# Output projection as seven block products, merge by pairs of row tiles, later modulations in attention

## The chip, the cores and the metric

The kernel runs on one core of a Trainium2 chip. The metric is the device time of one execution in microseconds (us); lower is better. Three runs of the kernel before gave a median of 2693.46 us. TensorE (PE in the profile) does the matrix products, VectorE (DVE), ScalarE (ACT) and GpSimd (POOL) the elementwise work, and SyncE's queue (SPq) issues most of the transfers from HBM.

## The reference

One layer over 1024 latent tokens (width 1024), with 256 context tokens that latent queries attend to. All of it is in fp32:

```python
x  = x + 0.5*ml[2] * swiglu(modulate(rms_norm(x, norm1_g), ml[0], ml[1]), ffn1_w_in, ffn1_w_out)
hx = modulate(rms_norm(x, norm2_g), ml[3], ml[4])
bg, cg, vc, q, k, v, gt = split(hx @ w_in)              # ctx gives k, v too
y_conv = bg * short_conv(cg * vc, conv_w)
o      = latent_attention(rope(norm(q)), k_all, v_all)  # 8 query heads, 2 kv heads of 128
g_conv, g_attn = split(sigmoid(gt))
x = x + ml[5] * ((g_conv*(y_conv @ w_bc) + g_attn*(o @ w_ba)) @ w_out)     # merge, output projection
x = x + 0.5*ml[8] * swiglu(modulate(rms_norm(x, norm3_g), ml[6], ml[7]), ffn2_w_in, ffn2_w_out)
return rms_norm(x, final_g)
```

`ml = split(silu(c) @ w_mod + b_mod)` are nine modulation vectors of 1024; each costs a pass over a 1024 x 1024 weight.

## The kernel before

**Products.** All activations lie transposed: 128 channels on the partitions, tokens along the free axis, in two halves of 512 tokens, C0 and C1. An fp32 product is made of three fp32r matmuls (`mm3`): both factors are cut by `split` into a high part (ACT makes the copy `hi`) and a low part (`src - hi`, on DVE unless another engine is named), and high x high, high x low and low x high are summed in one PSUM bank (`ps`, five banks).

**Block products.** The class `Winograd` multiplies 2x2 blocks with seven products in place of eight. A pair is two groups of 128 output channels. For each pair products 1 and 2 come first (`first`, `start`), then 6, 7, 4 (`second`), then 5 and 3 (`third`); each is 4 row tiles x 3 matmuls = 12 matmuls of 128x512. Its left-hand sides are sums of weight blocks (tiles `s`, summed on POOL, then split into tiles `wl`); its right-hand sides are kept split as tiles `r` by `keep`. Both FFNs and the mix `hx @ w_in` use it; the output projection does not. For the second FFN (`fast`), the generator `norm0` makes the normalised right-hand sides of half C0 (products 1, 2 and 3 read them) and `norm1` those of C1 and the mixed ones. Nine pairs (`AH3`) of products 1 and 2 run ahead, and behind them `second` starts, which needs the norm of C1.

**The stretch around the change.** Attention runs over 16 units (8 heads x 2 halves); each unit makes scores, exponentials, transposes (`pt`, turned into split tiles `pts`) and value products (`po`). `merge(j, ch)` then makes one row tile j of the merged branches for one half: 24 matmuls over the 8 heads, a gate multiply, an add, a split into `mh`/`ml`. There are 16 merges. The output projection loops over the halves and over eight output tiles d: `load_cols(w_out, d)` loads and splits 512 KB of weights, 24 matmuls follow, and x is updated. During the eight C1 tiles the C0 norm of FFN2 runs beside them (`first`, the generator of `norm0`).

**Later modulations.** `later_mod(6)` and `later_mod(7)` (the generator `late_steps`, 76 steps) load 256 KB tiles `rawm` of `w_mod`; DVE adds each, times one number of silu(c), into `macc` (32 such multiply-adds), and a split, a one-row product and a transpose end each half. Before, four steps run behind each of 14 merges and four behind each C0 tile of the projection.

**Order.** The source order is a priority; a scheduler with a timeline model sets the order of instructions on each engine. All instructions are issued by one helper, so the profile's line is always L90 and its groups are told apart by tile names. Buffers are rings: `raw` 3 x 512 KB, `wh` and `wl` 4 each, `ps` 5 banks; a transfer into a ring slot waits until the slot's last reader is done.

Of the kernel before, what the change touches and what calls it, by code (L numbers as in the profile page):

```python
# [9 lines left out]
F32 = mybir.dt.float32  # L10
# [8 lines left out]
P = 128  # L19
# [32 lines left out]
def tile_dit_layer(  # L52
# [29 lines left out]
    class Engine:  # L82


        def __init__(self, engine):
            self.engine = engine
# [36 lines left out]
    def ps_s(n=512):  # L123
        return psum.tile([P, 512], F32, tag="s", name=uniq("ps"), bufs=5)[:, :n]
# [362 lines left out]
    class Winograd:  # L487
# [3 lines left out]

        def __init__(self, xs, gain, mod, m, pairs, plain=False, ahead=3, side_from=None):
# [12 lines left out]
            self.source, self.ready = self.lefts(pairs, side_from), []  # L507

        def keep(self, i, k, src, lo_eng=None):

# [102 lines left out]
        def lefts(self, pairs, side_from):  # L613
# [29 lines left out]
            for j, (wa, wb) in enumerate(pairs):  # L643
# [16 lines left out]
                if side_from is not None and j == side_from - 1:  # L660
                    for wa, wb in pairs[:side_from]:
                        yield from map(parts, cols(wa) + cols(wb))

        def prefetch(self, n, lo_engines=(None, None)):
# [26 lines left out]
        def first(self):  # L691

            u, c = ttile("u"), ttile("c")
            act.copy(out=u, in_=self.product(1))
            dve.tensor_add(out=c, in0=u, in1=self.product(2))
            return u, c

        def start(self, norm):

# [807 lines left out]

    o_parts = [None] * NQ  # L1510

    def split_output(hd, *chunks):
        if o_parts[hd] is None:
            o_parts[hd] = atile("oh", dt=F32R), atile("ol", dt=F32R)
        a, b = chunks[0][1], chunks[-1][1] + 512
        split(q_f[hd][:, a:b], *(t[:, a:b] for t in o_parts[hd]))

    class Unit:
        def __init__(self, hd, ch):
# [82 lines left out]
            value()  # L1602
            yield

    m_hi, m_lo = {}, {}
    wa = {}

    def merge(j, ch):

        if j not in m_hi:  # L1610
            m_hi[j], m_lo[j] = atile("mh", dt=F32R), atile("ml", dt=F32R)
# [7 lines left out]
        terms = [  # L1619
            (w[0][:, k], w[1][:, k], *(t[:, o : o + 512] for t in o_parts[k])) for k in range(KD)  # L1620
        ]
# [5 lines left out]
        dve.tensor_add(out=ga, in0=ga, in1=z)  # L1627
# [43 lines left out]
    run(fill)  # L1671
    run(rest, 4)
    split_output(NQ - 2, C0, C1)
    split_output(NQ - 1, C0)
    merges = (step for j in range(2) for step in merge(j, C0))
    for _ in rest:
        run(merges, 2)
    run(merges)
    split_output(NQ - 1, C1)


    for j in range(KD):
        for ch in (C0, C1):
            if (j, ch) not in ((0, C0), (1, C0)):
                run(merge(j, ch))
                run(late_steps, 4)
    xs = Latents("x2")
    fast = Winograd(xs, None, modl, 6, column_pairs(ffn2_w_in[0], ffn_offsets), ahead=AH3)
    first = fast.norm0()
    for ch in (C0, C1):  # L1690
        o = ch[1]
        for d in range(KD):
            w = load_cols(w_out[0], d * P)
            load(xs(d, ch), xd[d, :, o : o + 512])
            ps = ps_s()
# [3 lines left out]
            dve.scalar_tensor_tensor(  # L1699
                out=xs(d, ch), in0=ps, scalar=modl[:, 40 + d : 41 + d], in1=xs(d, ch), op0=ALU.mult, op1=ALU.add  # L1700
            )
            if ch == C0:
                run(late_steps, 4)
                if d == KD - 1:
                    fast.gain = norm_gain("gain3", 6, "g3")["l"]
# [142 lines left out]
```

## Time and profile before

| what | before |
|---|---|
| median of 3 runs (lowest to highest) | 2693.46 us (2692.87 to 2695.69) |
| profiled execution, its own time | 2692.97 us |
| its span, mean granted TensorE clock | 2691.1 us, 0.995 |
| PE busy | 2646.4 us, 98% |
| DVE busy | 2016.0 us, 75% |
| ACT busy | 1178.8 us, 44% |
| POOL busy | 513.8 us, 19% |
| HBM traffic over the span | 138 GB/s |

The profile records one execution. Views used below: the totals by engine; groups of instructions by tile (count, busy us, mean ns, idle time before them and what ended it); stretches of the span with the busy time of each engine, the granted clock (PEclk, 1.00 is full speed) and the DMA share; the chain of work that ended last; and the timeline of one engine, a row for each run of like instructions (start, length, count, and in brackets the idle time before it with what ended it).

### The profile page before, as it was taken

Reading aid. Unit: us, or ns where it says so; the run is one execution under the profiler, and the core shown is the slowest. Engines: PE = TensorE matmul, PEld = TensorE weight load, DVE = VectorE, ACT = ScalarE, POOL = GpSimd, SP = SyncE. Lnnn points to the kernel's source line nnn. Section 1 sums busy time; section 2 is a strip of 40 time slices with the busy share of each in tenths; the row PEclk is TensorE's granted clock in tenths of the full one; section 3 lists DMA queues with packets and bytes.
Section 4 is the critical chain, followed back from the end, with each engine's and each line's share of the span. In section 5 each row is a group of like instructions: output and inputs, shape, how many; then the busy total and the mean of one; then the engine's idle time right before and its main releaser. Section 6 shows DMA issues by size and latency. Waiting matters only on the chain.

```text
span 2691.1 us, 36996 instructions
## 1 busy us (share of the span) xinstructions
PE 2646.4 (98%) x13437; PEld 2228.1 (83%) x13437; DVE 2016.0 (75%) x3363; ACT 1178.8 (44%) x2324; POOL 513.8 (19%) x403
## 2 busy tenths in 40 slices
PE   8999999999999999999999999999999999999998
PEld 5787899888778878888999888877888788888888
DVE  5788966888887899877487666785658886667885
ACT  6523454433454633333245666664236333334453
POOL 0144201221010044333023111000001442321200
PEclk9999999999999999999999999999999999999999
DMA  8565465346974345332213311011733552327841
GB/s 317 196 204 176 146 215 173 117 126 215 286 179 122 111 155 180 108 111 94 80 48 105 112 48 44 28 52 59 246 119 129 180 168 87 95 86 278 192 91 63
DMA packets 368206, 372.68 MB, mean 138 GB/s; under 512 B 18822, under 2 KB 257560, under 8 KB 368024
## 3 DMA queue, kind: packets, MB, share of 16 engines
q1 hardware_dynamic: 359000, 353.03, 39.9%
q0 software_dynamic: 9024, 17.30, 4.0%
q8 instruction: 105, 1.72, 0.3%
q14 instruction: 77, 0.63, 0.1%
HBM read 302.59 MB, written 67.63 MB: 138 GB/s over the span
## 4 chain that ended last, share of the span: by engine, by line
PE 91%; DVE 4%; DMA 2%; issue 2%; ACT 1%; POOL 0%; SPq 0%; DVEq 0%; POOLq 0%; ACTq 0%
PE ps L90 75%; PE pt L90 8%; PE po L90 7%; DMA rawm<-in_w_mod_dram 1%; DVE r L90 1%; DVE macc L90 0%; DMA ws<-in_ffn_w_out_dram 0%; DVE wl L90 0%; DVE nt L90 0%; DMA raw<-in_ffn_w_in_dram 0%; POOL s L90 0%; DVE uc L90 0%; DVE y L90 0%; DVE m L90 0%; DVE ol L90 0%
## 5 line engine op out<-in xcount | busy, mean ns | idle before, releaser
L90 PE MATMUL ps<-r,wl 128*128 128x512 f32 x5196 | 1206.5, 391 | 10.3 <-DVE wl L90 4.2
L90 PEld LDWEIGHTS ps<-r,wl 128*128 128x128 f32 x5196 | 974.1, 189 | 219.3 <-DVE wl L90 6.3
L90 ACT CAST wl<-s 128x512 fp32r<-128x512 f32 x254 | 156.7, 619 | 321.2 <-PE ps L90 218.7
L90 POOL TENSOR_TENSOR s<-raw 128x512 f32<-128x512 f32 x64 | 94.4, 1474 | 1051.2 <-DMA raw<-in_ffn_w_in_dram 630.7
L90 ACT CAST wl<-raw 128x512 fp32r<-128x512 f32 x287 | 177.5, 619 | 215.3 <-PE ps L90 153.9
L90 DVE TENSOR_TENSOR wl<-raw,wl 128x512 fp32r<-128x512 f32 x287 | 201.9, 705 | 62.1 <-ACT wl L90 60.3
L90 DVE TENSOR_TENSOR wl<-s,wl 128x512 fp32r<-128x512 f32 x254 | 230.4, 908 | 19.9 <-ACT wl L90 18.5
L90 POOL TENSOR_TENSOR s<-raw,s 128x512 f32<-128x512 f32 x64 | 103.8, 1623 | 361.1 <-DVE wl L90 361.1
L90 DVE SCALAR_TENSOR_TENSOR macc<-rawm,silu_c,macc 128x512 f32<-128x512 f32 x178 | 148.7, 852 | 25.0 <-DMA rawm<-in_w_mod_dram 24.3
L90 PE MATMUL ps<-wh,r 128*128 128x256 f32 x768 | 141.6, 285 | 0.0
L90 DVE TENSOR_TENSOR pts<-pt,pts 128x512 fp32r<-128x512 f32 x160 | 108.6, 686 | 41.4 <-ACT pts L90 40.2
L90 DVE TENSOR_TENSOR u<-u,ps 128x512 f32<-128x512 f32 x174 | 118.0, 678 | 27.8 <-PE ps L90 27.7
L90 ACT CAST pts<-pt 128x512 fp32r<-128x512 f32 x160 | 92.8, 592 | 89.5 <-PE pt L90 87.9
L90 DVE TENSOR_REDUCE m<-ps 128x1 f32<-128x512 f32 (+1 forms) x192 | 110.9, 595 | 26.0 <-PE ps L90 24.9
L90 ACT CAST rh<-hid 128x512 fp32r<-128x512 f32 x132 | 81.2, 620 | 107.1 <-PE ps L90 90.4
L90 PE MATMUL ps<-rh,wl 128*128 128x512 f32 x360 | 122.4, 390 | 2.8 <-ACT rh L90 2.8
L90 PEld LDWEIGHTS ps<-wh,r 128*128 128x128 f32 x768 | 120.6, 192 | 0.0
L90 PE MATMUL po<-pts,vh 128*128 128x512 f32 x256 | 111.7, 443 | 1.5 <-ACT pts L90 1.4
L90 PE MATMUL ps<-wl,r 128*128 128x256 f32 x384 | 108.8, 283 | 0.0
L90 PE MATMUL ps<-kl,qs 128*128 128x512 f32 x384 | 106.2, 397 | 0.4 <-ACT pc L90 0.4
L90 DVE TENSOR_TENSOR rl<-hid,rh 128x512 fp32r<-128x512 f32 x132 | 89.9, 684 | 21.7 <-PE ps L90 12.0
L90 ACT CAST wh<-raw 128x512 fp32r<-128x512 f32 (+1 forms) x85 | 67.9, 801 | 84.1 <-PE ps L90 57.7
(312 smaller groups left out, 5100.7 us busy)
## 6 DMA issues: line engine op xcount, KB each, us to landing
raw<-in_ffn_w_in_dram SPq DMA_DIRECT2D x130, 512.0 KB
raw<-in_ffn_w_out_dram SPq DMA_DIRECT2D x72, 512.0 KB
rawm<-in_w_mod_dram SPq DMA_DIRECT2D x136, 256.0 KB
raw<-in_w_in_dram SPq DMA_DIRECT2D x61, 512.0 KB
hid<-hd SPq DMA_DIRECT2D x40, 512.0 KB
ws<-in_ffn_w_out_dram POOLq DMA_DIRECT2D x30, 512.0 KB, 6.5
ucd<-uc SPq DMA_DIRECT2D x25, 512.0 KB
hd<-c SPq DMA_DIRECT2D x40, 256.0 KB
```

The lines of the kernel that those rows point to most:

```text
L90: inst = getattr(self.engine, name)(*args, **kw)
```

## The change

**The output projection** becomes a fourth use of `Winograd` (`proj`), with four pairs, output tiles i and i + 4. `lefts_apart` is the new list of left-hand sides: it makes 28 parts from 20 loads of 512 KB of `w_out`, with 24 sums on POOL, and gives every fourth part's low half to POOL. `start_all` runs products 1 and 2 of all four pairs, `second_of` products 6, 7 and 4 of each, and `third` products 5 and 3: 28 products of 12 matmuls. `add2` updates x and makes its squares. Half C0 of x is complete only when the last `second_of` is done, so `norm0` of FFN2 runs beside `third`.

**The merge** goes by pairs of row tiles (i, i + 4), C0 ahead of C1, and itself makes and keeps the seven right-hand sides (sums on DVE, one on POOL); the low halves of `w_ba` go to POOL. The attention outputs are kept split as one tile `op` for each head and half.

**Later modulations**: two steps run at two places of each of 15 attention units, three behind each merge outside attention and behind each step of the projection's first two phases; the gain of norm 3 is made ahead of the third phase.

```diff
     def split_output(hd, *chunks):
-        a, b = chunks[0][1], chunks[-1][1] + 512
-        split(q_f[hd][:, a:b], *(t[:, a:b] for t in o_parts[hd]))
+        for ch in chunks:
+            t = o_parts[hd, ch] = atile("op", (P, 2, 512), F32R)
+            split(q_f[hd][:, ch[1] : ch[1] + 512], t[:, 0], t[:, 1])
...
+        def lefts_apart(self, pairs):
...
+            for wa, _ in pairs:
+                yield from map(parts, halves(wa))
+            for wa, wb in pairs:
+                a, b = halves(wa), halves(wb)
+                s2, s3 = ttile("s2"), ttile("s3")
+                pool.tensor_add(out=s2, in0=b[0], in1=b[1])
+                pool.tensor_sub(out=s2, in0=s2, in1=a[0])
+                pool.tensor_sub(out=s3, in0=a[0], in1=b[0])
+                yield parts(s2)
+                yield parts(s3)
+                yield parts(b[1])
+            for wa, wb in pairs:
+                a, b = halves(wa), halves(wb)
+                s1, s2 = ttile("s1"), ttile("s2")
+                pool.tensor_add(out=s1, in0=b[0], in1=b[1])
+                pool.tensor_sub(out=s2, in0=s1, in1=a[0])
+                pool.tensor_sub(out=s2, in0=a[1], in1=s2)
+                yield parts(s1)
+                yield parts(s2)
...
     def merge(j, ch):
...
-            wa[j] = load_cols(w_ba[0], j * P)
+            wa[j] = load_cols(w_ba[0], j * P, pool)
...
-        split(ga, m_hi[j][:, o : o + 512], m_lo[j][:, o : o + 512])
+        if ch == C0:
+            out = raw_m[i][:, lower]
+            dve.tensor_add(out=out, in0=ga, in1=z)
+            proj.keep(1 + lower, i, out)
+        elif not lower:
+            dve.tensor_add(out=ga, in0=ga, in1=z)
+            dve.tensor_sub(out=t1, in0=ga, in1=raw_m[i][:, 0])
+            proj.keep(5, i, t1)
+        else:
+            dve.tensor_sub(out=t1, in0=ga, in1=t1)
+            pool.tensor_sub(out=b12, in0=ga, in1=b12)
...
             if n == 2:
                 run(fill, 1)
+                run(late_steps, 2)
...
-    for ch in (C0, C1):
-        for d in range(KD):
-            w = load_cols(w_out[0], d * P)
-            mm3(ps, [
-                (w[0][:, k], w[1][:, k], m_hi[k][:, o : o + 512], m_lo[k][:, o : o + 512]) for k in range(KD)
-            ])
-            if ch == C1:
-                fast.square(d)
-                if d in (0, 1):
-                    run(first, 1)
-                if d == 2:
-                    run(first)
+    proj.start_all(lambda: run(late_steps, 3))
+    for i, t in enumerate(proj.started):
+        add2(i, C0, t[:, 1])
+        add2(i + 4, C0, proj.second_of(t))
+        run(late_steps, 3)
+    run(late_steps)
+    fast.gain = norm_gain("gain3", 6, "g3")["l"]
+    for i, t in enumerate(proj.started):
+        run(first, 1 if i < 3 else None)
+        u, v = proj.third(t[:, 0], t[:, 1])
+        add2(i, C1, u)
+        add2(i + 4, C1, v)
```

**The order on the engines.** Three places. First PE, at the norm of half C0 for FFN2: `rs_y` is the reciprocal root that four matmuls spread over the partitions (`pt`), behind which DVE makes the right-hand sides `r`; in the rows of before, `mh`, `ml`, `wh`, `wl` are the output projection's factors. Before:

```order
L90 MATMUL pt_18980<-ident,rs_y_18931 128x128 x4
L90 MATMUL ps_19073<-mh_18434,wh_19067 128x512
L90 MATMUL ps_19073<-ml_18435,wh_19067 128x512
L90 MATMUL ps_19073<-mh_18434,wl_19068 128x512
L90 MATMUL ps_19109<-mh_17742,wh_19103 128x512
L90 MATMUL ps_19109<-ml_17743,wh_19103 128x512
```

The same place after the change; tiles `r_33` and `r_34` are right-hand sides of the projection, `r_3540` to `r_3542` the first of FFN2:

```order
L90 MATMUL pt_19172<-ident,rs_y_19106 128x128 x4
L90 MATMUL ps_19319<-r_3364_18248,wl_19228 128x512 x2
L90 MATMUL ps_19319<-r_3394_18419,wl_19228 128x512 x3
L90 MATMUL ps_19319<-r_3421_18582,wl_19228 128x512 x3
L90 MATMUL ps_19334<-r_3340_18121,wl_19276 128x512 x3
L90 MATMUL ps_19334<-r_3371_18294,wl_19276 128x512 x3
L90 MATMUL ps_19334<-r_3401_18465,wl_19276 128x512 x3
L90 MATMUL ps_19334<-r_3428_18628,wl_19276 128x512 x3
L90 MATMUL ps_19377<-r_3540_19183,wl_19363 128x512 x3
L90 MATMUL ps_19377<-r_3541_19188,wl_19363 128x512 x3
L90 MATMUL ps_19377<-r_3542_19193,wl_19363 128x512 x3
```

Before, 75 projection matmuls stand between the spread and FFN2's first product; after, 20 do.

Second PE again, at the norm of half C1: between this spread and the first of FFN2's products 6, 7 and 4 (on tiles that this norm makes). Before, the last rows ahead of that product and its first row:

```order
L90 MATMUL ps_19701<-r_3484_19011,wl_19634 128x512
L90 MATMUL ps_19701<-r_3485_19016,wl_19634 128x512 x3
L90 MATMUL ps_19701<-r_3486_19021,wl_19634 128x512 x3
L90 MATMUL ps_19701<-r_3487_19026,wl_19634 128x512 x3
L90 MATMUL ps_19722<-r_3549_19371,wl_19661 128x512 x2
```

After:

```order
L90 MATMUL ps_19850<-r_3555_19258,wl_19783 128x512
L90 MATMUL ps_19850<-r_3556_19263,wl_19783 128x512 x3
L90 MATMUL ps_19850<-r_3557_19268,wl_19783 128x512 x3
L90 MATMUL ps_19850<-r_3558_19273,wl_19783 128x512 x3
L90 MATMUL ps_19871<-r_3605_19520,wl_19810 128x512 x2
```

The spread stands 148 matmuls ahead of that product before and 111 ahead of it after (`pt_19302` and `pt_19451`), since fewer of the nine pairs' products are left when C1 of x is complete.

Third DVE, near the end of attention: `pts` are the split transposes that the value products wait for, `macc` the multiply-adds of the later modulations. Before:

```order
L90 TENSOR_TENSOR pts_17097<-pt_17092,pts_17097 128x512
L90 SCALAR_TENSOR_TENSOR macc_3284_17932<-rawm_17978,silu_c,macc_3284_17932 128x512
L90 SCALAR_TENSOR_TENSOR macc_3284_17932<-rawm_17981,silu_c,macc_3284_17932 128x512
L90 TENSOR_REDUCE rsum_17446<-rs_17625 128x1
L90 RECIPROCAL rinv_17888<-rsum_17446 128x4
L90 SCALAR_TENSOR_TENSOR macc_3284_17932<-rawm_17984,silu_c,macc_3284_17932 128x512
L90 TENSOR_TENSOR pts_17136<-pt_17131,pts_17136 128x512
```

After:

```order
L90 TENSOR_TENSOR pts_17717<-pt_17712,pts_17717 128x512
L90 TENSOR_SCALAR macc_3251_17678<-rawm_17679,silu_c 128x512
L90 TENSOR_TENSOR modl<-mcol_17675,bcol 128x4
L90 TENSOR_TENSOR pts_17728<-pt_17723,pts_17728 128x512
L90 SCALAR_TENSOR_TENSOR macc_3251_17678<-rawm_17790,silu_c,macc_3251_17678 128x512
L90 TENSOR_TENSOR pts_17739<-pt_17734,pts_17739 128x512
L90 SCALAR_TENSOR_TENSOR macc_3251_17678<-rawm_17793,silu_c,macc_3251_17678 128x512
```

Where three multiply-adds stood together ahead of a `pts`, now at most one does, and 24 of the 32 stand further up, between the transposes of attention.

More of the change, by code (lines that the diff above doesn't have):

```diff
@@ L487, in tile_dit_layer, with __init__ @@
     class Winograd:
-        def __init__(self, xs, gain, mod, m, pairs, plain=False, ahead=3, side_from=None):
+        def __init__(self, xs, gain, mod, m, pairs, plain=False, ahead=3, side_from=None, apart=False):
             self.xs, self.gain, self.mod, self.m, self.plain = xs, gain, mod, m, plain
@@ L506, in __init__ @@
             self.n_squares, self.accs = {}, {}
[L507 removed]
+            self.source, self.ready = (self.lefts_apart(pairs) if apart else self.lefts(pairs, side_from)), []
         def keep(self, i, k, src, lo_eng=None):
@@ L662, in lefts, with halves, parts @@
                         yield from map(parts, cols(wa) + cols(wb))
+        def lefts_apart(self, pairs):
+            def halves(src):
+                t = wpool.tile([P, SLOT], F32, tag="raw", name=uniq("raw"), bufs=3)
+                load(t[:].rearrange("p (k n) -> p k n", n=P), src.rearrange("(k p) n -> p k n", p=P))
+                return t[:, :512], t[:, 512:]
+            n_parts = [0]
+            def parts(src):
+                n_parts[0] += 1
+                t = wpool.tile([P, 2, 512], F32R, tag="wl", name=uniq("wl"), bufs=W_BUFS)
+                split(src, t[:, 0], t[:, 1], pool if n_parts[0] % 4 == 0 else None)
+                return t
+            for wa, _ in pairs:
[17 more added lines that the diff above has]
+                yield parts(s2)
         def prefetch(self, n, lo_engines=(None, None)):
@@ L696, in first, with start_all, second_of @@
             return u, c
+        def start_all(self, after=lambda: None):
+            for _ in range(self.n_ahead):
+                t = wpool.tile([P, 2, 512], F32, tag="wh", name=uniq("uc"), bufs=W_BUFS)
+                act.copy(out=t[:, 0], in_=self.product(1))
+                dve.tensor_add(out=t[:, 1], in0=t[:, 0], in1=self.product(2))
+                self.started.append(t)
+                after()
+        def second_of(self, t):
+            u, v, b = t[:, 0], t[:, 1], ttile("b")
+            dve.tensor_add(out=u, in0=u, in1=self.product(6))
+            dve.tensor_add(out=v, in0=u, in1=self.product(7))
+            dve.tensor_sub(out=b, in0=v, in1=self.product(4))
+            return b
         def start(self, norm):
@@ L1603, in seconds @@
             yield
-    m_hi, m_lo = {}, {}
-    wa = {}
+    wa, raw_m = {}, {}
+    proj = Winograd(
+        None, None, None, 0, [(w_out[0][:, i * P : (i + 1) * P], w_out[0][:, (i + 4) * P : (i + 5) * P]) for i in range(4)],
+        ahead=4, apart=True,
+    )
     def merge(j, ch):
-        if j not in m_hi:
-            m_hi[j], m_lo[j] = atile("mh", dt=F32R), atile("ml", dt=F32R)
+        i, lower = j % 4, j // 4
         if j not in wa:
-            wa[j] = load_cols(w_ba[0], j * P)
+            wa[j] = load_cols(w_ba[0], j * P, pool)
         w, o = wa[j], ch[1]
@@ L1674, in tile_dit_layer @@
     split_output(NQ - 1, C0)
-    merges = (step for j in range(2) for step in merge(j, C0))
+    merges = (step for j in (0, 4) for step in merge(j, C0))
     for _ in rest:
@@ L1679, in tile_dit_layer @@
     split_output(NQ - 1, C1)
-    for j in range(KD):
+    for i in range(4):
         for ch in (C0, C1):
-            if (j, ch) not in ((0, C0), (1, C0)):
-                run(merge(j, ch))
-                run(late_steps, 4)
+            for j in (i, i + 4):
+                if (i, ch) != (0, C0):
+                    run(merge(j, ch))
+                    run(late_steps, 3)
     xs = Latents("x2")
```

37 lines of the change are left out of this document (20 added, 17 removed).

## The prediction

> **What bounds the kernel now.** I read the totals by engine first, then the chain that ended last, then stretches of the span around the change.
>
> ```profile
> PE 2646.4 (98%) x13437; PEld 2228.1 (83%) x13437; DVE 2016.0 (75%) x3363; ACT 1178.8 (44%) x2324; POOL 513.8 (19%) x403
> PE 91%; DVE 4%; DMA 2%; issue 2%; ACT 1%; POOL 0%; SPq 0%; DVEq 0%; POOLq 0%; ACTq 0%
> ```
>
> PE is busy for 98% of the span and carries 91% of the chain. So a matmul taken away is worth its full time, unless something else is then late. The stretches (attention up to 1846, then merges, projection with the C0 norm, and the products ahead of FFN2's `second`):
>
> ```profile
> core 0: us, PE busy (x) PEld busy (x) DVE busy (x) ACT busy (x) POOL busy (x), PEclk, DMA share, GB/s
> 1440.00:1550.00 110.00, 109.63 (x590) 92.40 (x589) 78.90 (x169) 66.38 (x165) 27.27 (x27) 1.00 0.33 106
> 1750.00:1800.00 50.00, 48.25 (x276) 39.40 (x275) 44.22 (x93) 38.82 (x100) 0.00 (x0) 1.00 0.16 48
> 1800.00:1846.00 46.00, 40.32 (x224) 31.72 (x223) 28.53 (x43) 22.64 (x40) 0.00 (x0) 0.93 0.08 24
> 1870.00:1940.00 70.00, 70.00 (x310) 57.48 (x309) 46.50 (x69) 18.35 (x25) 0.00 (x0) 1.00 0.64 206
> 1940.00:2030.00 90.00, 90.00 (x404) 74.16 (x403) 54.98 (x85) 35.93 (x50) 0.00 (x0) 1.00 0.46 144
> 2030.00:2093.00 63.00, 61.40 (x279) 50.28 (x278) 54.23 (x86) 35.88 (x62) 12.04 (x7) 1.00 0.46 150
> ```
>
> Merges and projection (1870 to 2030) leave PE no idle time at all. PE waits at two places: the end of attention, and the end of the C1 norm (2030 to 2093, DVE busy 54.23 of 63).
>
> **The change part by part.** Sums are made against the profiled execution, 2692.97; the median is 0.5 above it.
>
> *Matmuls.* The projection's 384 matmuls become 28 products of 12, 336.
>
> ```profile
> L90 PE MATMUL ps<-mh,wl 128*128 128x512 f32 x128 | 49.9, 390 | 0.0
> L90 PE MATMUL ps<-mh,wh 128*128 128x512 f32 x128 | 49.9, 390 | 0.0
> L90 PE MATMUL ps<-ml,wh 128*128 128x512 f32 x128 | 49.8, 389 | 0.0
> 1918.29 27.23 PE ps L90 x120
> 2037.76 0.28 PE L90 MATMUL pt<-ones,sq_acc 128*128 128x1 f32 x2
> 2039.46 7.33 PE L90 MATMUL ps<-r,wl 128*128 128x512 f32 x31
> ```
>
> The mean of 390 ns overlaps its neighbours; a piece of the chain has the pace, 27.23 us for 120, so 0.2269 each. 48 fewer are −10.9. The merges keep their 16 x 24. The order has four more one-column matmuls for the norm (`pt<-ones`, two records each in the trace); eight of them took from 2037.76 to 2039.46, 0.21 each, so four are +0.9.
>
> *The C0 norm's cover.* Before, it ran ahead of 75 projection matmuls (17.0 us). Now 20 stand between its spread and FFN2's first product, and 7 more before the third right-hand side, 27 x 0.2269 = 6.1 us. DVE has 16 rows to do by then.
>
> ```profile
> 2047.27 1.28 DVE L90 TENSOR_TENSOR h<-x,pt 128x512 f32<-128x512 f32 x2 [0.42 <-PE pt L90]
> 2067.70 1.88 DVE L90 TENSOR_TENSOR r<-nt,r 128x512 fp32r<-128x512 f32 x3
> 2069.50 0.68 DVE L90 TENSOR_TENSOR wl<-raw,wl 128x512 fp32r<-128x512 f32 x1
> 2074.13 2.62 POOL L90 TENSOR_TENSOR s<-raw 128x512 f32<-128x512 f32 x1 [362.93 <-DMA raw<-in_ffn_w_in_dram]
> 2076.92 4.05 DVE L90 TENSOR_TENSOR r<-nt,r 128x512 fp32r<-128x512 f32 x3
> 2080.89 1.28 DVE L90 TENSOR_TENSOR wl<-s,wl 128x512 fp32r<-128x512 f32 x2
> 2090.93 0.73 PE L90 MATMUL ps<-r,wl 128*128 128x512 f32 x2 [0.27 <-DVE r L90]
> 2093.24 0.69 DVE L90 TENSOR_TENSOR r<-nt,r 128x512 fp32r<-128x512 f32 x1 [0.68 <-ACT r L90]
> 2093.26 7.91 PE L90 MATMUL ps<-r,wl 128*128 128x512 f32 x26 [1.60 <-ACT r L90]
> ```
>
> DVE's pace is (2069.50 − 2067.70)/3 = 0.60 a row, so 16 x 0.60 + 0.65 for the first wait on PE and ACT (0.42 to 0.68 here) = 10.2 us, late by 4.1: **+4.1**. Ends: 1.7 if the four `wl` rows among the 16 fall into waits (4 x 0.60 less); 6.3 if POOL's sums run beside, since three rows then took 4.05 for 1.88 (+2.2).
>
> *The C1 norm's cover.* Before, the last right-hand side of `second` was DVE's 64th row behind the spread, 2047.27 to 2093.24, 0.718 a row with POOL's sums beside part of it, and PE waited 0.27 + 1.60 = 1.87. After, it is the 59th row: 42.4 us. PE has 111 + 45 = 156 matmuls by then, 35.4 us (148 + 45 before). Late by 7.0, less 1.87: **+5.1**. Ends: −1.9 at the pace without POOL (59 x 0.60 = 35.4), +7.3 with one more group of three rows at POOL's side.
>
> [...]
>
> *The clock.* Behind the wait of 1.60, 26 matmuls took 7.91, and 26 x 0.2269 is 5.9: 2.0 lost to a slow clock. The C0 wait is new and as long; **+2.0**. Ends: 0 if no such drop follows, 4 for two. [...]
>
> *The weights of the third phase.* POOL makes three sums a pair, and a pair's second load can start only when the sums of the pair before have freed a `raw` slot.
>
> ```profile
> 2111.20 1.45 SPq L90 DMA_DIRECT2D raw<-in_ffn_w_in_dram  x2
> 2117.86 1.86 POOL L90 TENSOR_TENSOR s<-raw 128x512 f32<-128x512 f32 x1 [6.86 <-DMA raw<-in_ffn_w_in_dram]
> 2126.30 1.76 SPq L90 DMA_DIRECT2D raw<-in_ffn_w_in_dram  x2
> 2132.02 1.69 POOL L90 TENSOR_TENSOR s<-raw 128x512 f32<-128x512 f32 x1 [6.71 <-DMA raw<-in_ffn_w_in_dram]
> 2154.55 1.72 SPq L90 DMA_DIRECT2D raw<-in_ffn_w_in_dram  x2
> 2158.78 1.81 POOL L90 TENSOR_TENSOR s<-raw 128x512 f32<-128x512 f32 x1 [5.27 <-DMA raw<-in_ffn_w_in_dram]
> L90 POOL TENSOR_TENSOR s<-raw 128x512 f32<-128x512 f32 x64 | 94.4, 1474 | 1051.2 <-DMA raw<-in_ffn_w_in_dram 630.7
> L90 POOL TENSOR_TENSOR s<-s,raw 128x512 f32<-128x512 f32 x64 | 94.7, 1480 | 11.4 <-DVE macc L90 2.2 <-POOL s L90 1.4 <-issue 1.3
> ```
>
> From the issue's end to the sum's start, a load D takes 5.2, 4.0 or 2.5 us. POOL starts when product 16 frees a slot: a low half (1.5), three times three sums and a load (3 x (4.4 + D)), one more sum (1.5) and the two halves (1.2) give 17.4 + 3D until product 27 can start. PE gets there after 10 products, 120 x 0.2269 = 27.2. Late by 3D − 9.8: nothing at 2.5, 2.2 at 4.0, 5.8 at 5.2. I take the middle row: **+2.2**.
>
> *Attention.* The 32 multiply-adds of modulations 6 and 7 leave the merges and the projection, where PE never waited, and gain nothing there. At attention's end they stood in the way:
>
> ```profile
> 1800.67 0.75 DVE L90 SCALAR_TENSOR_TENSOR macc<-rawm,silu_c,macc 128x512 f32<-128x512 f32 x1 [0.62 <-DMA rawm<-in_w_mod_dram]
> 1802.78 0.75 DVE L90 SCALAR_TENSOR_TENSOR macc<-rawm,silu_c,macc 128x512 f32<-128x512 f32 x1 [1.08 <-DMA rawm<-in_w_mod_dram]
> 1803.45 1.28 DVE L90 TENSOR_TENSOR pts<-pt,pts 128x512 fp32r<-128x512 f32 x2
> 1801.70 0.50 PE L90 MATMUL po<-pts,vh 128*128 128x512 f32 x1 [1.10 <-ACT pts L90]
> 1804.19 1.12 PE L90 MATMUL pt<-ident,pl 128*128 128x128 f32 x4 [1.99 <-DVE pts L90]
> L90 DVE SCALAR_TENSOR_TENSOR macc<-rawm,silu_c,macc 128x512 f32<-128x512 f32 x178 | 148.7, 852 | 25.0 <-DMA rawm<-in_w_mod_dram 24.3
> ```
>
> DVE waits for a load with `pts` queued behind it, PE waits 1.10 + 1.99, and the clock falls to 0.93 for 46 us (3.2). All of this, −6.3, goes if the multiply-adds stand apart. 24 of them now lie in some 400 us of attention, 24 x 0.852 = 20.4 us, raising DVE's share there by 0.05. At a share of 0.72 (1440 to 1550) PE lost 0.37 in 110, over 400 us 1.5; at 0.88 (1750 to 1800) it lost 1.75 in 50, over 400 us 14. The first is nearer: +1.5, together **−4.8** (−6.3 to +7.7). Each step also puts a 256 KB load on SP's queue ahead of attention's fillers; DMA is busy for 0.16 to 0.33 there, so I cost it at nothing, and a late one is inside the upper end.
>
> In the merges DVE does 46.5 of 70 us, and the new sums replace the low halves of `w_ba`, now on POOL, which is idle there; hidden. If that cover went, it would be the 0.60 of a row each time.
>
> *Sum:* −10.9 + 0.9 + 4.1 + 5.1 + 2.0 + 2.2 − 4.8 = −1.4, so 2691.6 in a profiled execution, 2692.1 as a median. Three quarters of the saved matmuls are given back at the two norms, which the projection's matmuls used to cover.
>
> **The rivals.**
> - *The norms keep pace (faster).* DVE's rows go at 0.60, without POOL beside them: C0 norm 1.7, C1 norm −1.9, no drop of the clock, no late weights: −10.9 + 0.9 + 1.7 − 1.9 − 4.8 = −15.0, 2678.5; with the middle of each term instead of its lower end, about 2685. For it: the row pace of 0.60 holds for most of 2047 to 2074. Against it: POOL's sums start ahead of both norms' ends.
> - *POOL's sums hold DVE (slower).* In the third phase sums, splits and norm run together, so that all upper ends come at once: 6.3, 7.3, two drops of the clock (4), D = 5.2 (5.8): −10.9 + 0.9 + 6.3 + 7.3 + 4.0 + 5.8 − 4.8 = +8.6, 2702.1. It decides from the point where a pair's 4.4 + D on POOL passes its 24 x 0.2269 = 5.4 us on PE, and grows with each pair. For it: D of 4.0 is past that point; against: a head start of four products.
> - *The moved multiply-adds reach PE (slower).* A transfer in attention is late, and `pts` stand behind it as at 1802.78: 14 in place of 1.5, 2704.6. For it: 25 us of DVE idleness by `rawm`; against: PE without a wait at shares up to 0.72.
> - That the change doesn't do what it says is ruled out for the matmuls: the order has 48 fewer.
>
> **How the numbers follow.** The forecast gets 0.40, the norms that keep pace 0.32, POOL's sums 0.16, the multiply-adds 0.12. The forecast's own range is 2686 to 2698. A measurement tells 0.2%, 5.4 us, from no change: faster is below 2688.1, slower above 2698.9. Faster: 0.11 of the forecast and 0.31 of the first rival, 0.42. Slower: 0.07 of the forecast, 0.12 and 0.09 of the others, 0.28. Within: 0.30. The range, 2679 to 2704, leaves out the first rival's lower end and the last one's upper end.
>
> **What would show it.** Right: PE at 48 fewer matmuls; no wait for `pts` near attention's end and its clock at 1.00 there; a wait of 3 to 5 us ahead of FFN2's first product, released by `r`; a wait of some 7 us at its first `second` products, also `r`; a wait of about 2 us for `wl` in the projection's last pair. Wrong: no such waits (the first rival), waits for `wl` that grow from pair to pair with POOL busy (the second), PE waiting for `pts` behind `macc` throughout attention (the third), or PE waiting inside the merges.

## The result, and the profile after

The changed kernel is slower: median 2712.21 us of 6 runs (2708.99 to 2718.99) against 2695.38 us of 6 runs of the kernel before; ratio 1.0067, 95% interval 1.0054 to 1.008. The forecast was 2692.1, with a range that ended at 2704; no rival had a time above 2704.6. The profiled execution took 2714.7 us, 2.5 above its median.

The page of the changed kernel (span, totals by engine, chain by engine):

```profile
span 2712.8 us, 37140 instructions
PE 2651.1 (98%) x13397; PEld 2225.8 (82%) x13397; DVE 2054.4 (76%) x3418; ACT 1187.5 (44%) x2359; POOL 588.6 (22%) x446
PE 84%; DVE 7%; DMA 3%; issue 3%; ACT 2%; POOL 1%; SPq 0%; DVEq 0%; POOLq 0%; ACTq 0%
```

PE has fewer instructions and yet is busy for longer (2646.4 before): some of them ran at a slower clock (mean granted clock 0.991 against 0.995). PE's idle time (span less busy) grew from 44.7 to 61.7. DVE and POOL have more to do, and DVE's part of the chain grew from 4% to 7%.

The same five stretches in both kernels, cut at instructions that both have: the first score matmul on context keys, the last value product, the last merge matmul, FFN2's first product, the first of FFN2's products 6, 7 and 4, and 200 matmuls later. First the kernel before, then the changed one (columns as in the prediction: start:end, length, busy us of PE, PEld, DVE, ACT, POOL, granted clock, DMA):

```profile
1457.80:1866.20 408.40, 399.86 (x2169) 332.37 (x2168) 275.79 (x565) 251.81 (x610) 41.50 (x25) 0.99 0.19 59
1866.20:1939.70 73.50, 73.50 (x326) 60.37 (x325) 50.05 (x73) 21.33 (x29) 0.00 (x0) 1.00 0.60 195
1939.70:2029.40 89.70, 89.70 (x403) 73.90 (x402) 54.38 (x84) 35.44 (x49) 0.00 (x0) 1.00 0.46 146
2029.40:2080.60 51.20, 51.20 (x237) 42.69 (x236) 42.90 (x75) 31.97 (x55) 5.61 (x3) 1.00 0.44 144
2080.60:2130.20 49.60, 47.74 (x201) 38.30 (x201) 42.85 (x58) 16.03 (x28) 19.19 (x13) 0.97 0.57 174
```

```profile
1459.90:1879.00 419.10, 402.73 (x2156) 330.92 (x2155) 286.86 (x594) 256.19 (x623) 49.53 (x28) 0.99 0.21 65
1879.00:1956.10 77.10, 77.10 (x341) 63.62 (x340) 55.65 (x75) 22.71 (x35) 18.41 (x8) 1.00 0.48 154
1956.10:2037.80 81.70, 79.64 (x358) 64.94 (x356) 63.71 (x85) 27.07 (x48) 48.72 (x32) 1.00 0.53 158
2037.80:2101.40 63.60, 55.39 (x238) 44.27 (x237) 55.03 (x96) 42.47 (x71) 3.64 (x3) 0.95 0.46 147
2101.40:2152.30 50.90, 48.66 (x200) 39.03 (x201) 44.25 (x60) 17.55 (x31) 20.42 (x14) 0.93 0.54 169
```

Attention and merges together: 481.9 before, 496.2 after, +14.3 (taken together, since the boundary between them moved by some merge matmuls). The projection: −8.0. The start of FFN2, where its C0 norm and then its C1 norm are waited for: +12.4. The next 200 matmuls: +1.3. That is 20.0 of the 21.7 between the two spans. What lies ahead of attention is the same program in both, and 2.1 longer in this execution.

The waits in the last three stretches, from PE's timeline of the changed kernel:

```profile
2002.97 8.98 PE L90 MATMUL ps<-r,wl 128*128 128x512 f32 x38 [0.22 <-ACT wl L90]
2012.35 7.33 PE L90 MATMUL ps<-r,wl 128*128 128x512 f32 x31 [0.16 <-DVE wl L90]
2032.81 0.62 PE L90 MATMUL pt<-ident,rs_y 128*128 128x128 f32 x4 [1.69 <-DVE rs_y L90]
2038.70 0.73 PE L90 MATMUL ps<-r,wl 128*128 128x512 f32 x2 [0.40 <-DVE r L90]
2045.30 16.99 PE L90 MATMUL ps<-r,wl 128*128 128x512 f32 x63 [3.21 <-DVE r L90]
2101.38 0.94 PE L90 MATMUL ps<-r,wl 128*128 128x512 f32 x2 [3.69 <-ACT wl L90]
2103.39 16.79 PE L90 MATMUL ps<-r,wl 128*128 128x512 f32 x62 [1.07 <-ACT wl L90]
2121.34 8.91 PE L90 MATMUL ps<-r,wl 128*128 128x512 f32 x38 [1.17 <-DVE wl L90]
```

For the projection's own weights PE waits 0.22 and 0.16, no more. For the C0 norm it waits 1.69 for the reciprocal root; then 7 matmuls (1.6 us of work) take from 2037.8 to 2045.3, 5.9 lost, and the next 63 take 16.83 in place of 14.3, 2.5 lost to a slow clock: 10.1 in all (of the 5.9, 4.5 are waits for `r`; the rest is matmuls that each start alone or by two, 0.50 for one and 0.73 for two where 0.2269 each is the pace). At the C1 norm it waits 3.69, 1.07 and 1.17, each time for weights (`wl`), not for right-hand sides.

In attention the new waits look like this one at its start (timelines of DVE, ACT, PE): a multiply-add `macc` stands at the head of DVE's queue until its load is there, 3.89 us; behind it stands `nm`, which the exponential `pc` waits for, which the score matmuls wait for. Whether the load is what costs here is tested below (no_mod_loads).

```profile
1469.81 0.48 DVE L90 TENSOR_SCALAR macc<-rawm,silu_c 128x512 f32<-128x512 f32 x1 [3.89 <-DMA rawm<-in_w_mod_dram]
1470.21 0.15 DVE L90 TENSOR_REDUCE nm<-m 128x1 f32<-128x3 f32 x1
1470.39 0.47 ACT L90 ACTIVATE pc<-ps,nm 128x256 f32<-128x256 f32 x1 [3.57 <-DVE nm L90]
1471.01 0.63 PE L90 MATMUL ps<-kc,qs 128*128 128x256 f32 x3 [2.07 <-ACT pc L90]
```

### The profile page after: what moved, and what is told of

Same layout as the page of the kernel before. It is cut to its first block, busy times and chain, and to the rows that moved or that the text cites. A ratio compares the mean times of both kernels' runs of the same rounds, so it can differ in the third digit from the quotient of the medians.

```text
span 2712.8 us, 37140 instructions
## 1 busy us (share of the span) xinstructions
PE 2651.1 (98%) x13397; PEld 2225.8 (82%) x13397; DVE 2054.4 (76%) x3418; ACT 1187.5 (44%) x2359; POOL 588.6 (22%) x446
## 4 chain that ended last, share of the span: by engine, by line
PE 84%; DVE 7%; DMA 3%; issue 3%; ACT 2%; POOL 1%; SPq 0%; DVEq 0%; POOLq 0%; ACTq 0%
PE ps L90 69%; PE pt L90 7%; PE po L90 7%; DMA rawm<-in_w_mod_dram 1%; POOL s L90 1%; DVE wl L90 1%; DVE r L90 1%; DVE macc L90 1%; DVE uc L90 1%; DVE nt L90 0%; DVE xb L90 0%; DVE m L90 0%; DMA ws<-in_ffn_w_out_dram 0%; DMA raw<-in_ffn_w_in_dram 0%; DVE pts L90 0%
## 5 line engine op out<-in xcount | busy, mean ns | idle before, releaser
L90 PE MATMUL ps<-r,wl 128*128 128x512 f32 x5532 | 1290.7, 393 | 18.9 <-ACT wl L90 7.1
L90 PEld LDWEIGHTS ps<-r,wl 128*128 128x128 f32 x5532 | 1040.2, 189 | 244.6 <-ACT wl L90 10.9
L90 ACT CAST wl<-s 128x512 fp32r<-128x512 f32 x270 | 166.4, 619 | 349.0 <-PE ps L90 220.3
L90 ACT CAST wl<-raw 128x512 fp32r<-128x512 f32 x299 | 184.9, 619 | 223.5 <-PE ps L90 159.0
L90 POOL TENSOR_TENSOR s<-raw 128x512 f32<-128x512 f32 x72 | 104.5, 1451 | 764.4 <-DMA raw<-in_ffn_w_in_dram 373.6
L90 DVE TENSOR_TENSOR wl<-s,wl 128x512 fp32r<-128x512 f32 x266 | 241.1, 907 | 28.0 <-ACT wl L90 26.3
L90 DVE TENSOR_TENSOR wl<-raw,wl 128x512 fp32r<-128x512 f32 x296 | 208.9, 707 | 63.6 <-ACT wl L90 60.9
L90 POOL TENSOR_TENSOR s<-raw,s 128x512 f32<-128x512 f32 x68 | 110.4, 1623 | 364.1 <-DVE wl L90 363.8
L90 POOL TENSOR_TENSOR s<-s,raw 128x512 f32<-128x512 f32 x72 | 107.2, 1489 | 12.2 <-issue 2.6
L90 POOL TENSOR_TENSOR s<-raw,raw 128x512 f32<-128x512 f32 x68 | 102.4, 1506 | 18.8 <-DVE wl L90 12.4
```

The costliest lines, as they stand in the source:

```text
L90: inst = getattr(self.engine, name)(*args, **kw)
```

## The experiments

Each kernel was timed against the kernel before on the same chip. The excess over the kernel before is (ratio − 1) x 2695.4; by the intervals each is good to 2 to 4 us, and the difference of two of them to some 4.

| kernel | median us | ratio (95% interval) | excess us |
|---|---|---|---|
| changed | 2712.21 | 1.0067 (1.0054 to 1.008) | +18.1 |
| attn_as_before | 2707.68 | 1.0045 (1.0033 to 1.0058) | +12.1 |
| mods_only | 2712.04 | 1.0058 (1.0044 to 1.0073) | +15.6 |
| no_mod_loads | 2712.22 | 1.0055 (1.0043 to 1.0068) | +14.8 |
| cover_doubled | 2713.28 | 1.0066 (1.0054 to 1.0079) | +17.8 |
| before_no_mods | 2689.20 | 0.9972 (0.9962 to 0.9983) | −7.5 |
| after_no_mods | 2695.97 | 1.0002 (0.9993 to 1.0011) | +0.5 |
| after_mods_pool | 2707.72 | 1.0042 (1.0029 to 1.0054) | +11.3 |
| before_late_start | 2692.85 | 0.9987 (0.9978 to 0.9996) | −3.5 |
| narrow_mods | 2702.71 | 1.0028 (1.0018 to 1.0039) | +7.5 |
| half_mods | 2704.32 | 1.0031 (1.0021 to 1.0041) | +8.4 |
| no_third_sums | 2688.03 | 0.9974 (0.9964 to 0.9985) | −7.0 |

### attn_as_before: the modulations out of attention again

```diff
-                run(late_steps, 2)
...
-                    run(late_steps, 3)
+                    run(late_steps, 4)
```

> The changed kernel, but the two steps of the later modulations at each place of attention are taken out again and four (not three) steps run behind each merge and each step of the projection; the order then has no multiply-add of modulations 6 and 7 before the last pts. Theory (DVE's queue head: a multiply-add that waits for its 256 KB load holds nm and pts behind it, and PE waits for these): the 10.9 us that attention lost against the kernel before go, and the 6.3 at its end that the kernel before loses too: 2712.2 - 10.9 - 6.3 = 2695, at the kernel before or 2 to 3 us from it, with PE's waits between 1460 and 1880 us down from 16 us to under 4. Rival 1 (the loss lies in the projection and its norms alone; attention's waits are made up later): no change, 2712. Rival 2 (only the waits that are new go): 2701.

It got only 6.0 of its 18.1 back. Attention itself did as the theory says, 398.8 us against 419.1 (PE idle there for 5.3, under 4 expected). But the steps now fall on the merges (82.7 against 77.1) and on the projection (90.5 against 81.7, no faster than the 384 matmuls of before). PE there waits for the modulations' own split (`acch`) and for `wl`:

```profile
1926.80 0.59 PE L90 MATMUL pt<-acch,ones_r 128*1 128x512 f32 x1 [2.29 <-ACT acch L90]
1971.47 8.97 PE L90 MATMUL ps<-r,wl 128*128 128x512 f32 x32 [2.52 <-DVE wl L90]
```

DVE did 80.5 of 90.5 us in this projection. The new projection has no room for the modulations that the old one hid.

### mods_only: the modulations moved, and nothing else

```diff
             if n == 2:
                 run(fill, 1)
+                run(late_steps, 2)
```

> The kernel before, with only the two steps of the later modulations at two places of each attention unit added; merge and projection as before. All 32 multiply-adds of modulations 6 and 7 then stand in attention, in four groups of eight. Theory (queue head): attention loses about what the changed kernel lost there, 8 to 12 us, and the rest stays: 2695.4 + 10 = 2705. Rival (attention's loss needs the other edits, or is made up later): 2695 plus or minus 2.

Slower by 15.6, more than expected. In attention the waits stand at the places of the changed kernel, 1.74 for `pc` at the start and 2.62 for `nm` in the middle; its 428.5 us there hold all 32 multiply-adds, eight of them in the tail. The move alone does this harm; no other edit is needed.

```profile
1471.77 0.63 PE L90 MATMUL ps<-kc,qs 128*128 128x256 f32 x3 [1.74 <-ACT pc L90]
1752.64 1.11 PE L90 MATMUL pt<-ident,pc 128*128 128x128 f32 x4 [2.62 <-DVE nm L90]
```

### before_no_mods and after_no_mods: the two projections without the modulations

```diff
-    mix_steps, late_steps, last_steps = later_mod(5), (step for m in (6, 7) for step in later_mod(m)), later_mod(8)
+    mix_steps, late_steps, last_steps = later_mod(5), iter(()), later_mod(8)
+    dve.memset(modl[:, 48:64], 0.25)
```

> The kernel before without the later modulations 6 and 7: no loads, no multiply-adds, no small products (a constant stands in for their values). Theory (the kernel before hides them in merges and projection, but for attention's end): only the waits at attention's end go, 5 to 6 us: 2691. Rival (they are hidden altogether, attention's end waits for something else): 2696 to 2697.

> The changed kernel without the later modulations 6 and 7, as above: what is left is the seven-product projection, with its merges, alone. Theory (two costs: the moved multiply-adds cost attention some 20 us, 419.1 against 398.8; the projection alone gives back its 10 saved us at the C0 norm): 2712.2 - 20 = 2692, within 3 us of before_no_mods. Rival 1 (DVE is what is short, so that without the modulations the norms keep pace too): 2680 to 2684, below before_no_mods by 8 or more. Rival 2 (the projection is itself the loss): 2700 or more.

−7.5 and +0.5. This splits the result: the modulations cost 17.6 in the changed kernel and 7.5 in the kernel before, 10.1 more; the seven-product projection by itself costs 8.0 more than the old one, although it has 48 matmuls (10.9 us) less. The first figure is good to some 5 us, the second to some 4. The profiled executions agree: without the modulations, projection and the two stretches behind it are 6.7 longer in the changed kernel; the modulations cost attention and merges 20.8 there (496.2 against 475.4) and 5.6 in the kernel before (481.9 against 476.3). The expected 2691 and 2692 were 2 and 4 us off, and the projection's own loss was expected at under 3. Its waits at the norms are those of the changed kernel to 0.1 us (3.21 for `r`, 3.67 for `wl`), so the modulations have no part in them.

### cover_doubled: more matmuls ahead of the norm

```diff
-            for k in range(4):
-                self.terms(ps, w, i, k)
+            for _ in range(2 if self.twice and i in (3, 5) else 1):
+                for k in range(4):
+                    self.terms(ps, w, i, k)
```

> The kernel attn_as_before, with each of the eight products of the projection's third phase run twice over (the second pass overwrites the first): 96 matmuls more, 96 x 0.2269 = 21.8 us of PE work that covers the C0 norm and asks nothing of the other engines. Theory (cover: PE waits 6.2 us for the C0 norm and loses 3.1 to a slow clock behind it because 20 matmuls are too few to hide it): both vanish, so the time grows by 21.8 - 9.3 = 12.5 over attn_as_before, and PE waits nowhere between the last projection product and the first FFN2 product. Rival (DVE and POOL set the pace of this stretch whatever PE does, the C1 norm included): growth under 5. Second rival (the waits are not at the norm): growth of 21.8.

96 matmuls, 21.8 us, added 5.7 (17.8 against 12.1). The waits for `r` at the C0 norm are gone (one of 1.14 for the reciprocal root stays), and at the C1 norm PE waits 1.3 in all, where attn_as_before waits 4.4:

```profile
2029.63 32.35 PE L90 MATMUL ps<-r,wl 128*128 128x512 f32 x142
```

142 matmuls now run without a gap where the changed kernel stood. FFN2's start, up to its first products 6, 7 and 4, and the 200 matmuls behind it, first in attn_as_before, then here:

```profile
2035.90:2096.90 61.00, 54.57 (x238) 43.49 (x236) 54.67 (x95) 41.70 (x71) 4.17 (x3) 0.94 0.47 152
2096.90:2147.90 51.00, 48.92 (x201) 39.10 (x202) 45.28 (x60) 16.40 (x29) 20.37 (x14) 0.93 0.55 166
```

```profile
2053.70:2105.00 51.30, 51.30 (x238) 42.74 (x237) 42.47 (x74) 31.01 (x53) 6.03 (x3) 1.00 0.44 144
2105.00:2153.50 48.50, 47.16 (x202) 37.05 (x201) 41.65 (x56) 16.61 (x29) 19.02 (x13) 1.00 0.54 169
```

12.2 us come back here, idle time and slow clock both, and the stretches are as short as in the kernel before (51.2 and 49.6). So the theory's mechanism holds, though not its 12.5: it left out what more cover does for the C1 norm. The growth of 5.7 is nearest to the first rival's, but the trace doesn't bear that rival out: PE is busy for all of the 51.30, so that nothing else sets its pace there. 21.8 less 12.2 is 9.6; from the projection's start to the end of the 200 matmuls the profiled executions differ by 8.1.

### no_third_sums: the projection without POOL's last twelve sums

```diff
-                pool.tensor_add(out=s1, in0=b[0], in1=b[1])
-                pool.tensor_sub(out=s2, in0=s1, in1=a[0])
-                pool.tensor_sub(out=s2, in0=a[1], in1=s2)
-                yield parts(s1)
-                yield parts(s2)
+                yield parts(b[0])
+                yield parts(a[1])
```

> The kernel after_no_mods with the third phase's twelve sums on POOL left out: the raw weight halves stand in for them (those products' values are left out), loads, splits and matmuls stay. In the changed kernel DVE's rows beside these sums took some 9.5 us more than alone, 5 of them behind the last product of the second phase. Theory (POOL's sums hold DVE, and so make the C0 norm later than 20 matmuls can hide): the 10 us lost at the C0 norm fall to 5 or less, 2696.0 - 5 to 8 = 2688 to 2691. Rival (the chain of the norm itself, from x over squares and reciprocal root to r, is longer than 96 matmuls, whatever POOL does): less than 2 us gained, 2694 to 2696.

−7.0 against +0.5: 7.5 gained, the upper half of the expectation. In the changed kernel DVE's rows beside POOL look like this (timelines of DVE and POOL); 0.68 is the length of such a DVE row alone:

```profile
2024.18 1.74 DVE L90 TENSOR_TENSOR sq_acc<-sq_acc,sq 128x512 f32<-128x512 f32 x1 [1.22 <-ACT sq L90]
2025.84 1.78 DVE L90 TENSOR_TENSOR wl<-s,wl 128x512 fp32r<-128x512 f32 x1
2028.87 0.68 DVE L90 TENSOR_TENSOR wl<-s,wl 128x512 fp32r<-128x512 f32 x1
2025.44 1.63 POOL L90 TENSOR_TENSOR s<-s,raw 128x512 f32<-128x512 f32 x1
2027.14 1.63 POOL L90 TENSOR_TENSOR s<-raw,s 128x512 f32<-128x512 f32 x1
```

The two `uc` rows at 2027.61, which read one input from PSUM, took 1.27 together beside the last of these sums, no more than alone (1.28 for the two at 2032.58).

Without the sums PE no longer waits for `rs_y`, and the spread stands 32 matmuls ahead of the one long wait left, in place of some 27; PE still waits 3.18 there:

```profile
2009.84 0.60 PE L90 MATMUL pt<-ident,rs_y 128*128 128x128 f32 x4
2010.19 7.72 PE L90 MATMUL ps<-r,wl 128*128 128x512 f32 x32
2021.09 16.36 PE L90 MATMUL ps<-r,wl 128*128 128x512 f32 x65 [3.18 <-ACT r L90]
```

In the profiled executions the gain lies where it should: the projection falls from 81.9 to 79.0, FFN2's start from 63.5 to 59.6, and the next 200 matmuls stay at 50.9. The sums are nearly the whole of the projection's net loss of 8.0. But with the 10.0 that its matmuls save, the projection gives back some 18, and of these the sums are under half. What remains is the wait of 3.18, one of 3.21 at the C1 norm and the slow clock behind both (65 matmuls in 16.36 us, then six in 2.93, where the pace of 0.2269 gives 14.7 and 1.4), and cover_doubled shows that more matmuls ahead would hide them. That the sums cost this by holding DVE is read from DVE's rows; no run kept the sums and freed DVE of them.

### no_mod_loads, half_mods, narrow_mods: what of the modulations costs attention

```diff
+                if m in (6, 7):
+                    raw = ident[:, None, :].to_broadcast([P, 4, P])
...
+                        if k:      # narrow_mods: 16 columns; half_mods: 256
+                            acc, raw = acc[:, 0, :16], ident[:, :16]
```

> The changed kernel, but the multiply-adds of modulations 6 and 7 read a resident constant in place of their loads: the same DVE instructions at the same places, without the 32 loads of 256 KB (the modulations' values are left out). Theory (it is the wait for the load at DVE's queue head): attention's waits go as if the steps were not there, 2712.2 less 10 to 15 = 2697 to 2702. Rival (it is the DVE time of the multiply-adds, 27 x 0.85 = 23 us, that delays nm and pts): 2710 to 2712, with the waits at their places.

> The kernel no_mod_loads with all but the first multiply-add of each half of a modulation narrowed to 16 of its 512 columns: as many instructions, at about the same places, but some 0.65 us of DVE time less each (28 of them). It left 411.7 us of attention where the kernel without modulations has 398.8. Theory (the DVE time itself comes out of attention, at nearly its full length): attention at 400 to 403 us, about 9 us below no_mod_loads. Rival (what costs is the changed order and the split and small products behind each half, not the time of the multiply-adds): attention stays at 409 to 412.

> As narrow_mods, but each of the 28 multiply-adds works on 256 of its 512 columns: about half its DVE time. With 512 columns (no_mod_loads) the median was 2712.2, with 16 columns 2702.7, though the profiled executions of both showed attention at 411 us. Theory (the DVE time counts): in between, 2706 to 2709. Rival (what counts is the order, and one of the two medians comes from where the clock's slow stretches fall): at one of the two ends, under 2704 or over 2711.

From the changed kernel down: without the loads 3.3 less, within the intervals; at half the width 6.4 less; at 16 columns 0.9 less; without the modulations 7.0 less. So my theory of the load at the queue's head, which the rows at 1469.81 seem to show, falls as the main cause: with the loads gone other waits take their place, and at attention's start PE still waits 1.66 where it waited 2.07. The rival, DVE time, accounts for a part, but by the times not in proportion: half the time of the multiply-adds costs 6.4, the other half 0.9. Much of the 6.4 is clock: the mean granted clock of the timed runs was 0.9914 in no_mod_loads, 0.9933 in half_mods and 0.9926 in narrow_mods, and 0.0019 of 2704 us is 5.1, an estimate, and at most that, since PE is idle in a part of the slow stretches (in the changed kernel it was busy for 5.75 of the 6.82 us at half clock from 2101.73 on). With the clock taken out in this way the two halves cost 1.3 and 2.8. And 7.0 remain with multiply-adds of almost no length. PE's longer waits in attention stand at the same places; three of no_mod_loads, then two of narrow_mods:

```profile
1470.84 0.62 PE L90 MATMUL ps<-kc,qs 128*128 128x256 f32 x3 [1.66 <-ACT pc L90]
1557.41 0.63 PE L90 MATMUL pt<-ident,pl 128*128 128x128 f32 x4 [1.42 <-DVE pts L90]
1745.39 0.66 PE L90 MATMUL pt<-ident,pl 128*128 128x128 f32 x4 [2.02 <-DVE pts L90]
```

```profile
1554.94 0.63 PE L90 MATMUL pt<-ident,pl 128*128 128x128 f32 x4 [1.42 <-DVE pts L90]
1742.20 0.66 PE L90 MATMUL pt<-ident,pl 128*128 128x128 f32 x4 [2.51 <-DVE nm L90]
```

Ahead of the last of these, DVE in narrow_mods runs the end of one modulation half and the split of the next between `m` and `nm`: `modl` 0.72, a `macc` of 16 columns that takes 1.33 (0.22 a little later), and `accl` 1.49 where the mean is 0.72:

```profile
1735.29 0.72 DVE L90 TENSOR_TENSOR modl<-mcol,bcol 128x4 f32<-128x4 f32 x1
1735.93 1.33 DVE L90 SCALAR_TENSOR_TENSOR macc<-ident,silu_c,macc 128x16 f32<-128x16 f32 x1
1740.05 1.49 DVE L90 TENSOR_TENSOR accl<-macc,acch 128x512 fp32r<-128x512 f32 x1
```

Open: the profiled executions gave attention 411.7, 408.7 and 411.1 us for 512, 256 and 16 columns, and do not show the 6.4 that the timed runs show. The changed kernel's 419.1 is 7.4 above no_mod_loads, 5.1 of it three stretches of slow clock that no_mod_loads does not have in attention. What brings the slow clock, and which of order, split and small products makes the 7.0, isn't settled.

### after_mods_pool: the multiply-adds on POOL

```diff
+                    if m in (6, 7):
+                        pool.tensor_scalar(out=acc if k == 0 else raw, in0=raw, scalar1=s, scalar2=None, op0=ALU.mult)
+                        if k:
+                            pool.tensor_add(out=acc, in0=acc, in1=raw)
```

> The changed kernel with the multiply-adds of modulations 6 and 7 made on POOL, at the same places, as a multiply and an add. Theory (DVE's in-order queue: the time of the multiply-adds and their loads delays nm and pts): attention goes back to about 400 us, 2712.2 - 17 = 2695 to 2698. Rival (loads and POOL's hold on DVE cost as much): 2708 to 2713.

6.8 gained, not 17: attention took 410.8 us, not 400. Out of DVE's way, the modulations still cost over half of what they did; their split and small products stay in the queues, and POOL now multiplies and adds there, 1.69 and 1.34 us each, beside DVE. The two were not told apart.

### before_late_start: the kernel before, modulations out of attention's end

```diff
                 run(merge(j, ch))
-                run(late_steps, 4)
+                if j >= 3:
+                    run(late_steps, 5)
...
-                run(late_steps, 4)
+                run(late_steps, 5)
```

> The kernel before, with the later modulations' steps begun only behind the merges of row tile 3, five at a time: no multiply-add of modulations 6 and 7 stands before the last pts any more. Theory (attention's end waited for them, and the projection's 384 matmuls hide them all): faster than the kernel before by 4 to 6, about 2691. Rival (they then wait in merges and projection, as in attn_as_before where PE waited there for acch): 2697 or slower.

Faster than the kernel before by 3.5 (interval 1 to 6), and the fastest full kernel of all here. 4 to 6 were expected. Attention fell from 408.4 to 404.1 (404.0 without any later modulations, in before_no_mods), merges (73.5) and projection (89.7) stayed as they were, without a wait. One of the two waits at attention's end remains, so it was not the multiply-adds':

```profile
1802.01 0.50 PE L90 MATMUL po<-pts,vh 128*128 128x512 f32 x1 [1.21 <-ACT pts L90]
```

## Why the prediction was wrong

The step that failed is the last of the sum, **attention**: −4.8 forecast, +14.3 measured. It failed twice. The gain was put at 6.3 by reading both end waits as the multiply-adds'; only about 4 go (before_late_start), and a wait of 1.21 stays there. And the price of 24 multiply-adds in attention was read from DVE's busy share (1.5). The runs show 20.8 in its place: 496.2 us of attention and merges with the modulations, 475.4 without (after_no_mods); in the kernel before the modulations cost 5.6 there. Even the upper row, 14, was too low. In attention DVE sits in a ring PE → ACT → DVE → PE, as the rows at 1469.81 show from DVE on; that its place in the order counts there, and not its mean load, is how I read the waits that narrow_mods keeps, and no run shows it by itself. The rival "the moved multiply-adds reach PE" had the direction and stood at 0.12; its time, 2704.6, still held the gain of 6.3, and its late transfers are at most a part (3.3 without any loads).

The other terms, in us, forecast and measured in the profiled execution:

| step | forecast | measured |
|---|---|---|
| matmuls, with the norm's four | −10.0 | −10.0 by count |
| C0 norm's wait | +4.1 | +7.6 (1.69 + 5.9) |
| clock behind it | +2.0 | +2.5 |
| weights of the third phase | +2.2 | +0.4 |
| C1 norm, with the clock behind it | +5.1 | +5.0 (3.7 + 1.3) |
| attention and merges | −4.8 | +14.3 |

- Right: that the saved matmuls would be given back at the norms, which they used to cover (cover_doubled), and the clock's price.
- C0 norm: the size was off, at its start. The pace was right: the 16 rows from the first `h` to the third right-hand side, 2035.58 to 2045.2, took 0.60 each. But the spread itself came 1.69 late, and behind it five rows of the projection (`uc`, `wl`) still stood ahead of the first `h`, which started 2.8 after the spread, not 0.65. POOL's last sum ended at 2028.8, so the sums made DVE late ahead of the spread, where the forecast did not count. In no_third_sums the first `h` starts 0.63 behind the spread.

```profile
2032.58 1.28 DVE L90 TENSOR_TENSOR uc<-uc,ps 128x512 f32<-128x512 f32 x2
2035.58 1.28 DVE L90 TENSOR_TENSOR h<-x,pt 128x512 f32<-128x512 f32 x2
2044.56 1.29 DVE L90 TENSOR_TENSOR r<-h,r 128x512 fp32r<-128x512 f32 x2
```

- C1 norm: right in size by luck, by another cause. PE waited for the weights of the first products, not for `r`. POOL's timeline has the first sum for them at 2094.64, released by a row `r` of DVE, 3 us before PE ran out of work (2101.38 − 3.69); before, it stood at 2074.13, 6.5 ahead of that product at 2080.6. In the kernel, sums and the norm's `nt` and `h` take their tiles from one ring of 11 (`ttile`), so a sum has to wait until DVE has read an older one. That it is DVE's lateness that passes on to the weights is read from this row, and no run took it apart.

```profile
2094.64 1.68 POOL L90 TENSOR_TENSOR s<-raw 128x512 f32<-128x512 f32 x1 [63.84 <-DVE r L90]
```

- Weights of the third phase: the loop of loads and sums kept up; no wait there grew from pair to pair.
- The rival "POOL's sums hold DVE" was right in its mechanism (DVE rows of 1.74 and 1.78 us beside the sums, 0.68 alone) and too small alone; two rivals came true at once, which the chances, split over single cases, had no room for.
- Two slips in the working change nothing: 0.37 lost in 110 us is 1.35 in 400, not 1.5, and 4.1 + 5.1 is over four fifths of the 10.9, not three quarters.

Beside the profile, the kernels without modulations give the two parts of the 18.1 by timed runs: 8.0 for the projection, 10.1 for the modulations' new place.

## What to carry to other kernels

Before work is taken from a saturated engine, ask what was hidden under that work: here 384 matmuls covered a norm and a modulation pass, and the 336 that replaced them covered neither, while beside their sums on POOL the rows of the engine that the norm needs grew longer (on DVE 1.78 us where one alone takes 0.68). An engine's idle share need not be room for more work when it stands inside a dependence ring: here some 20 us of multiply-adds, in 400 us of attention where DVE was busy for 0.68, came with a loss of 20 us; leaving the moved work out altogether, in both versions, shows in one run each what its place costs. And ask whether a step can start later instead of elsewhere: modulation steps begun four merges later beat both kernels.

## What the runs showed of the hardware

TensorE's clock dropped to half (PEclk 0.50) in pieces: in the changed kernel's trace nine of 3.41 us and two of 6.83, besides one that ran on past the end; in the kernel before four of 3.41 and one of 6.83, besides one at the end. Of two waits of about 2 us in attention, 2.07 at 1471 and 2.25 at 1496, one was followed by a piece. Four stretches of the changed kernel: the first holds the first 1.33 us of the wait of 2.07, the second the whole wait of 2.25, the third and the fourth are pieces:

```profile
1466.86:1470.27 3.41, 2.08 (x10) 1.39 (x8) 0.46 (x2) 0.00 (x0) 0.00 (x0) 1.00 0.50 154
1494.16:1497.57 3.41, 1.16 (x6) 0.98 (x7) 1.32 (x3) 1.78 (x6) 1.28 (x1) 1.00 0.76 226
1497.57:1500.98 3.41, 3.41 (x10) 2.62 (x9) 2.86 (x8) 2.71 (x6) 1.31 (x1) 0.50 0.21 81
2101.73:2108.55 6.82, 5.75 (x14) 3.95 (x13) 6.82 (x9) 2.85 (x6) 2.61 (x2) 0.50 0.15 56
```

Behind the wait of 2.07 came none; behind the one of 2.25 came one piece, in which PE was busy for all of the 3.41 us, so 1.7 lost; behind that of 3.69 at 2101 came 6.82 us at half clock, with PE busy for 5.75, so 2.9 lost. PE was busy for 1.16 of the 3.41 us ahead of the drop at 1497.57, and for 2.08 of the 3.41 us in the first row, which no drop followed.

The starts of the eleven pieces in the changed kernel's trace lie whole multiples of 3.413 us apart (from 1497.57 to 2101.73 it is 177 of them). What decides whether a wait brings a piece was not shown: no run moved a wait against these times.
